# A down product that walks its chunk pairs in a rolling order, with partial sums added in DRAM

## The chip, the cores and the metric

The kernel runs on one core of a Trainium2 chip. The metric is the device time of one execution in microseconds. A core has a matrix engine (TensorE, PE in the profile; PEld is its weight load), a vector engine (VectorE, DVE), a scalar engine (ScalarE, ACT), a general engine (GpSimd, POOL), and a sync engine (SyncE, SP) that here only issues DMAs. Work memory is SBUF, TensorE writes to PSUM, and the large tensors lie in DRAM. A DMA can be issued by SP, ACT or POOL; each issuing engine starts its DMAs in its own program order.

## The reference

A trunk of two layers over 1024 tokens of 1024 channels, all in fp32. Each layer adds to the residual x a mixer, a cross-attention into 256 memory tokens, and a feed-forward block:

```python
def swiglu(h, w_gate, w_up, w_down):
    return (jax.nn.silu(h @ w_gate) * (h @ w_up)) @ w_down

x = x + swiglu(rms_norm(x, g_ffn[layer]), w_gate[layer], w_up[layer], w_down[layer])
```

The hidden width is 2816. The change concerns the last product, with w_down (2816 x 1024), and its addition to x, in both layers.

## The kernel before

**Layout.** Activations lie channel-major: a chunk is 128 channels by 1024 tokens. The hidden activations are 22 chunks, which the gate and up stage stores to the DRAM tensor pd. The residual has 8 chunks; between stages it lies in the DRAM tensor xs.

**Products.** Two neighbouring chunks form a Pair (lines 277 to 326), and its two chunks with the two halves of the tokens are a 2 x 2 block matrix; a Unit (lines 201 to 245) is the matching piece of a weight matrix, n pairs of 128-row blocks by 256 output channels. Seven products take the place of the eight of a 2 x 2 block product (function seven, line 1716): operand i of the unit and operand i of every pair, each a sum or difference of blocks. Each operand is kept as two numbers, a rounded high part (ScalarE, line 241 for weights, 318 for activations) and the rest (VectorE, line 409), so that a product takes three matmuls of 128 x 128 by 128 x 512 per pair (line 397): high by high, high by rest, rest by high. The sums and differences are made at line 232 for weights, on the engine named by the unit's argument adds, and at line 307 on POOL for activations. A unit of n pairs takes 7 splits (128n columns) and 4 sums; a pair takes 7 splits of 512 columns and 4 subtractions.

**Visits.** I call one unit with its pairs a visit. It accumulates in four PSUM banks and gives a quarter each for two output chunks. Its results go out in one of two ways: onto_x (line 1778) adds each product's bank to the resident residual chunk on VectorE, 8 adds per visit; collected (line 1741) builds the two output chunks in fresh tiles, by 3 ScalarE copies (lines 1756, 1762, 1764) and 4 VectorE adds (line 1754), and hands each quarter to a function. Gate and up use collected, the down product onto_x.

**The down product.** DOWN (line 32) splits the 11 chunk pairs into groups of 3, 3, 3 and 2. For each group the loop at line 1862 visits the four output pairs (of two chunks each, 256 channels), so a layer has 16 visits. The residual's 8 chunks are loaded from xs by x_back (line 1880), two of them in the gate and up stage and six in down_start (line 1841), into the "a" half of the raw arena, and stay there to the end. In the last group each finished quarter is passed on: in layer 1 to emit (line 2021), which transposes it on TensorE and stores it to the output; in layer 0, when a visit is done, to chunk_done (line 617), which normalises two chunks into the input of the odd mixer of layer 1 (lines 624, 625, 629, 632, 633). Its products (dense, line 665) then read chunk 0 first and chunk 7 last.

**Order of the work.** Every visit adds seven tasks with the operands they need. run (line 423) goes through the tasks and, ahead of each, fetches and makes operands of later tasks in the order of first use. Three numbers limit it: la, the columns made ahead of use; raws, the operand sources fetched and not yet begun; and f_reserve, which a unit's fetch must leave free in the raw arena. Raw data live in the F arena (16,384 columns, half "a" and half "b"), made operands in the R arena (35,840 columns); a buffer is reused once its last reader is done. A pair's chunks are loaded by SP from pd (line 1856) into "b" only, w_down by SP (line 222), also into "b" only. A tile scheduler then fixes each engine's program order from these priorities and its own timeline, and sets the waits.

Of the kernel before, what the change touches and what calls it, by code (L numbers as in the profile page):

```python
# [14 lines left out]
P = 128  # L15
S = 1024
# [15 lines left out]
DOWN = ((0, 1, 2), (3, 4, 5), (6, 7, 8), (9, 10))  # L32
# [244 lines left out]
class Pair:  # L277


    def __init__(self, load=None, home="ab", adds="gpsimd"):  # L280
        self.load, self.home, self.adds = load, home, adds
# [52 lines left out]
class Trunk:  # L334
    def __init__(self, tc, ctx, args):
# [48 lines left out]
        self.f_reserve = 0  # L384
        self.pS, self.pT, self.pM, self.pF = PSETS
# [231 lines left out]
    def chunk_done(self, gname, layer, k):  # L617
# [9 lines left out]
        if k == 0:  # L627
# [8 lines left out]
    def stats(self):  # L636
# [10 lines left out]
        self.ssq.free()  # L647

# [1092 lines left out]
    def collected(self, quarter, where="ba"):  # L1741
# [54 lines left out]
    def ffn(self, layer, pairs, finish=None, opening=None, emit=None):  # L1796
# [33 lines left out]

        self.add(start)
        for j in range(NF // 2):
# [14 lines left out]
        def down_end():  # L1847
            self.la, self.reserve = 3072, 0

        for n, group in enumerate(DOWN):  # L1850
            last = n == len(DOWN) - 1

            def load(f):
                def fn(t0, t1):
                    for e, t in enumerate((t0, t1)):
                        nc.sync.dma_start(out=t.ap, in_=self.pd[layer, (f + e) * P:(f + e + 1) * P, :])
                return fn
            home = "b" if last and finish else "ab"
            ps = [Pair(load(2 * j), home) for j in group]
            if last and opening:  # L1860
                self.add(opening)
            for mp in range(KD // 2):
                u = Unit(wd, group[0] * 256, len(group), mp * 256, "b", "b" if last and finish else "ba", "gpsimd")
                lead = [u.parts[0]] + [o for p in ps[:-1] for o in p.ops] if mp == 0 else ()
                if last and mp == 1:
                    self.add(down_end)
                quarter = None
                if last:
                    seen = []

                    def quarter(m, half, seen=seen):
                        if emit:
# [209 lines left out]
```

## Time and profile before

| | us |
|---|---|
| median of three runs | 2492.29 (2490.76 to 2493.66) |
| the profiled execution, its time | 2492.48 |
| its span on the core | 2490.7 |
| PE busy in the span | 2369.1 |
| DVE busy | 1722.8 |
| ACT busy | 1026.5 |
| POOL busy | 853.0 |

The mean granted TensorE clock was 0.973. The time of an execution lies 1.8 us over the span of its instructions. In the profile's names, arena_f and arena_r are the F and R arenas, psum_t is PSUM; a row of the grouped view reads: line, engine, operation, output<-inputs, output shape<-input shape, count, then busy us, mean ns of one, and the idle time of the engine just ahead of these, with what ended it. In the table of stretches each engine has its busy us and, in brackets, its instructions; then come the granted clock, the mean share of the 16 DMA engines in use, and GB/s. In the views of waits each row is: who waited, for whom, us in total, times, longest us.

### The profile page before, as it was taken

What the parts mean: (1) busy time and instruction counts of PE and PEld (TensorE: products, weight loads), DVE (VectorE), ACT (ScalarE), POOL (GpSimd) and SP (SyncE); (2) the same over time, 40 slices, a digit from 0 to 9 for tenths busy, and PEclk for the clock granted to TensorE, in tenths of its full rate; (3) what the DMA queues carried; (4) which work ended last, traced back from release to release, by engine and by line L of the source; (5) the groups of instructions that cost most, each with busy time, mean ns of one, the idle gap of its engine ahead of it and who ended that gap; (6) DMA issues with size and microseconds to landing.
All of it is one profiled execution on the core that took longest, in us unless ns stands there. A gap on an engine that the chain in (4) does not pass through costs nothing. (4 is left out here: it accounts for less than half of the span.)

```text
span 2490.7 us, 30370 instructions
## 1 busy us (share of the span) xinstructions
PE 2369.1 (95%) x11246; PEld 1978.2 (79%) x11246; DVE 1722.8 (69%) x2449; ACT 1026.5 (41%) x1886; POOL 853.0 (34%) x849
## 2 busy tenths in 40 slices
PE   7999999999899999998899999999799999989998
PEld 7998889888678888876677888888588887767776
DVE  5456367855686676689989643545876767589887
ACT  5355366645543333343335221244533333344332
POOL 6551233243531112136654300132721111146551
PEclk9999999999889999999999999999799999999999
DMA  7345345421231312243222121110321231243322
GB/s 233 124 144 172 94 119 141 132 76 35 102 102 51 102 60 85 93 139 110 93 89 81 60 59 35 59 43 18 118 85 68 93 102 51 74 164 102 102 87 74
DMA packets 175836, 234.83 MB, mean 94 GB/s; under 512 B 7200, under 2 KB 145528, under 8 KB 175688
## 3 DMA queue, kind: packets, MB, share of 16 engines
q1 hardware_dynamic: 171856, 220.10, 28.1%
q0 software_dynamic: 3648, 12.75, 1.4%
q8 instruction: 88, 1.44, 0.2%
q14 instruction: 60, 0.49, 0.1%
q10 hardware_dynamic: 184, 0.05, 0.0%
HBM read 176.11 MB, written 56.75 MB: 93 GB/s over the span
## 5 line engine op out<-in xcount | busy, mean ns | idle before, releaser
L397 PE MATMUL psum_t<-arena_r 128*128 128x512 f32 (+4 forms) x10304 | 2293.3, 381 | 99.1 <-DVE arena_r L409 43.4
L397 PEld LDWEIGHTS psum_t<-arena_r 128*128 128x128 f32 (+1 forms) x10304 | 1867.5, 191 | 473.9 <-DVE arena_r L409 67.1
L409 DVE TENSOR_TENSOR arena_r<-arena_f,arena_r 128x512 fp32r<-128x512 f32 (+4 forms) x839 | 739.0, 904 | 303.5 <-ACT arena_r L241 153.6
L241 ACT CAST arena_r<-arena_f 128x512 fp32r<-128x512 f32 (+2 forms) x532 | 288.8, 563 | 565.1 <-PE psum_t L397 402.3
L1806 POOL TENSOR_TENSOR arena_f<-arena_f 128x512 f32<-128x512 f32 x88 | 135.1, 1538 | 656.3 <-ACT arena_f L1805 656.1
L307 POOL TENSOR_TENSOR arena_f<-arena_f 128x512 f32<-128x512 f32 x120 | 184.1, 1550 | 120.4 <-DMA arena_f<-pd 58.2
L232 POOL TENSOR_TENSOR arena_f<-arena_f 128x384 f32<-128x384 f32 (+1 forms) x128 | 148.2, 1166 | 103.6 <-DVE arena_r L409 51.7
L1785 DVE TENSOR_TENSOR arena_f<-psum_t,arena_f 128x512 f32<-128x512 f32 x256 | 167.7, 680 | 15.7 <-PE psum_t L397 15.0
L318 ACT CAST arena_r<-arena_f 128x512 fp32r<-128x512 f32 x210 | 123.6, 617 | 124.9 <-POOL arena_f L307 62.4
L232 DVE TENSOR_TENSOR arena_f<-arena_f 128x512 f32<-128x512 f32 x176 | 136.0, 778 | 55.6 <-DMA arena_f<-w_up 34.2
L1754 DVE TENSOR_TENSOR arena_f<-psum_t,arena_f 128x512 f32<-128x512 f32 x176 | 119.9, 685 | 33.9 <-PE psum_t L397 28.3
L527 ACT CAST arena_r<-arena_f 128x1024 fp32r<-128x1024 f32 (+1 forms) x57 | 59.0, 1042 | 109.9 <-PE psum_t L397 99.5
L409 DVE TENSOR_TENSOR arena_r<-psum_t,arena_r 128x512 fp32r<-128x512 f32 (+3 forms) x124 | 84.7, 703 | 24.9 <-ACT arena_r L1596 8.7
L1805 ACT ACTIVATE arena_f<-arena_f 128x512 f32<-128x512 f32 x88 | 55.6, 632 | 99.7 <-DVE arena_f L1804 99.2
L633 POOL TENSOR_TENSOR arena_f<-arena_f 128x1024 f32<-128x1024 f32 x21 | 60.3, 2870 | 87.0 <-ACT arena_f L632 79.7
L1259 POOL TENSOR_SCALAR arena_f<-arena_f,small 128x640 f32<-128x640 f32 (+6 forms) x64 | 49.4, 780 | 108.6 <-DVE small L1258 104.6
L1813 DVE TENSOR_TENSOR arena_f<-arena_f 128x512 f32<-128x512 f32 x88 | 73.9, 841 | 3.3
L1804 DVE TENSOR_TENSOR arena_f<-arena_f 128x512 f32<-128x512 f32 x88 | 70.7, 804 | 0.8
L420 POOL TENSOR_TENSOR small<-small,mhalf 128x4 f32<-128x4 f32 (+1 forms) x64 | 64.3, 1005 | 5.2
L1705 POOL TENSOR_TENSOR arena_f<-arena_f 128x512 f32<-128x512 f32 x28 | 43.7, 1571 | 50.7 <-ACT arena_f L1704 50.2
L1948 POOL TENSOR_TENSOR arena_f<-arena_f 128x1024 f32<-128x1024 f32 x4 | 9.6, 2392 | 140.9 <-DVE arena_f L1900 136.1
L1254 ACT ACTIVATE arena_f<-psum_t,small 128x640 f32<-128x640 f32 (+6 forms) x64 | 47.5, 744 | 23.0 <-DVE small L1252 20.1
(177 smaller groups left out, 1390.9 us busy)
## 6 DMA issues: line engine op xcount, KB each, us to landing
arena_f<-w_gate SPq DMA_DIRECT2D x22, 1024.0 KB
arena_f<-w_up SPq DMA_DIRECT2D x22, 1024.0 KB
pd<-arena_f SPq DMA_DIRECT2D x44, 512.0 KB
arena_f<-pd SPq DMA_DIRECT2D x44, 512.0 KB
arena_f<-w_down SPq DMA_DIRECT2D x24, 768.0 KB
arena_f<-xs SPq DMA_DIRECT2D x32, 512.0 KB
arena_r<-qk SPq DMA_DIRECT2D x48, 256.0 KB
xs<-arena_f SPq DMA_DIRECT2D x24, 512.0 KB
```

The costliest lines, as they stand in the source:

```text
L232: getattr(T.nc, self.adds).tensor_tensor(out=out, in0=a, in1=b, op=what)
L241: T.nc.scalar.copy(out=hv, in_=src)
L307: getattr(T.nc, self.adds).tensor_tensor(out=out, in0=a, in1=b, op=ALU.subtract)
L318: T.nc.scalar.copy(out=h.ap, in_=src)
L397: self.nc.tensor.matmul(out=out, lhsT=lhsT, rhs=rhs, start=start, stop=stop, skip_group_check=again)
L409: getattr(self.nc, eng).tensor_tensor(out=out, in0=src, in1=high, op=ALU.subtract)
L420: self.nc.gpsimd.tensor_tensor(out=out, in0=in_, in1=self.mhalf[:, 0:in_.shape[-1]], op=ALU.pow)
L1754: nc.vector.tensor_tensor(out=o, in0=bank[q].ap, in1=o if other is None else other, op=ALU.add)
L1785: nc.vector.tensor_tensor(out=o, in0=bank[q].ap, in1=o, op=ALU.add)
L1804: nc.vector.tensor_tensor(out=q, in0=q, in1=r, op=ALU.mult)
L1806: nc.gpsimd.tensor_tensor(out=q, in0=q, in1=r, op=ALU.mult)
L1813: nc.vector.tensor_tensor(out=c[j].ap[:, o], in0=c[j].ap[:, o], in1=s.ap[:, o], op=ALU.mult)
```

## The change

The four fixed groups go. The visits now take the output pairs in turn: visit n (from -3) works on output pair n mod 4 and on the chunk pairs n to n+3, as far as they exist, so that each visit takes up one new chunk pair and lets go of one, and each chunk pair is met by all four output pairs in four visits running. In layer 1 that makes 14 visits of 1, 2, 3, eight times 4, 3, 2 and 1 pairs. In layer 0 only nine chunk pairs are rolled (visits of 1, 2, 3, six times 4, 3, 2 and 1 pairs), and four last visits take pairs 9 and 10 to the output pairs 1, 2, 3, 0.

A visit that isn't the last for its output pair collects its two chunks in fresh tiles and adds them onto xs in DRAM by a DMA with accum_op on POOL's queue, one per chunk. The last visit of an output pair adds onto the residual chunks as before; x_back loads these two chunks ahead of the last visits, one output pair at a time, in place of all eight at the start.

Moved along with this: the units of w_down no longer name "gpsimd" for their sums, so that Unit's default, VectorE, makes them; chunk pairs and most units may be loaded into both halves of the F arena, and a pair's fetch honours f_reserve too; la in the stage is 8192 (was 16384), f_reserve 4096 (was 0), raws 4 (was 2, set for gate and up). The first visit of a group no longer names operands of the whole group as its lead. chunk_done starts its sum of squares with whichever chunk comes first, since chunks 0 and 1 now come last in layer 0. collected takes its second tile at product 4, not at product 0.

```diff
     def fetch(self, T, must):                       # Pair
         if self.load is None:
             return True
+        if not must and sum(map(T.F.room, self.where)) - 3 * S < T.f_reserve:
+            return False
         got = []
         for cols in (S, S, 512, 512):
-            b = T.F.alloc(cols, "b")
+            b = T.F.alloc(cols, self.where)
...
             if i == 0:                              # collected
-                st["c"] = [self.F.get(S, where) for _ in range(2)]
+                st["c"] = []
+            if i in (0, 4):
+                st["c"].append(self.F.get(S, where))
...
+        rolled = 9 if finish else 11                # ffn
+        visits = [(n % 4, [j for j in range(n, n + 4) if 0 <= j < rolled]) for n in range(-3, rolled)]
+        if finish:
+            visits += [(mp, list(range(rolled, NF // 2))) for mp in (1, 2, 3, 0)]
...
-            if j == 9:
-                self.add(lambda: self.x_back(0, 2))
 
         def down_start():
             self.rbc.free()
-            self.x_back(2, KD)
-            self.la, self.f_reserve = 16384, 0
+            self.x = [None] * KD
+            self.la, self.f_reserve, self.raws = 8192, 4096, 4
         self.add(down_start)
...
+        ps = [Pair(load(2 * j), "b" if finish and j >= rolled else "ab", "gpsimd", "ba") for j in range(NF // 2)]
+
+        def onto_xs(m):
+            def fn(j, half, c):
+                if (j, half) in ((1, 0), (0, 1)):
+                    def keep():
+                        nc.gpsimd.dma_start(out=self.xs[(m + j) * P:(m + j + 1) * P, :], in_=c[j].ap,
+                                            accum_op=ALU.add)
+                        c[j].free()
+                    self.defer(keep)
+            return fn
...
-            for mp in range(KD // 2):
-                u = Unit(wd, group[0] * 256, len(group), mp * 256, "b", "b" if last and finish else "ba", "gpsimd")
...
+        for n, (mp, group) in enumerate(visits):
+            last = all(v[0] != mp for v in visits[n + 1:])
+            late = n >= len(visits) - 6
+            u = Unit(wd, group[0] * 256, len(group), mp * 256, "b" if late else "ba",
+                     "b" if finish and late else "ba")
...
+            if last:
+                nxt = [v[0] for v in visits[n:]]
+                if n + 4 == len(visits):
+                    self.add(lambda mp=mp: self.x_back(2 * mp, 2 * mp + 2))
+                if n + 1 < len(visits):
+                    self.add(lambda q=nxt[1]: self.x_back(2 * q, 2 * q + 2))
+                if n + 3 == len(visits):
                     self.add(down_end)
...
+            self.seven(u, [ps[j] for j in group], self.onto_x(2 * mp, last_part(mp)) if last else
+                       self.collected(onto_xs(2 * mp), "b" if late else "ba"))
```

More of the change, by code (lines that the diff above doesn't have):

```diff
@@ L31 @@
 AF_COLS = 16 * 1024
-DOWN = ((0, 1, 2), (3, 4, 5), (6, 7, 8), (9, 10))
 class Buf:
@@ L277, with __init__ @@
 class Pair:
-    def __init__(self, load=None, home="ab", adds="gpsimd"):
-        self.load, self.home, self.adds = load, home, adds
+    def __init__(self, load=None, home="ab", adds="gpsimd", where="b"):
+        self.load, self.home, self.adds, self.where = load, home, adds, where
         self.t = [None, None]
@@ L384, in __init__ @@
         self.f_reserve = 0
+        self.ssq = None
         self.pS, self.pT, self.pM, self.pF = PSETS
@@ L647, in stats @@
         self.ssq.free()
+        self.ssq = None
     def spread(self):
@@ new lines, in load, with fn @@
+        def load(f):
+            def fn(t0, t1):
+                for e, t in enumerate((t0, t1)):
+                    nc.sync.dma_start(out=t.ap, in_=self.pd[layer, (f + e) * P:(f + e + 1) * P, :])
+            return fn
[8 more added lines that the diff above has]
+                    self.defer(keep)
+            return fn
```

40 lines of the change are left out of this document (14 added, 26 removed).

## The prediction

> **What bounds the kernel now.** I read the page first, then a table of four stretches: 200 us out of each gate and up stage (800 to 1000, 1850 to 2050) and the two down products with what runs into them (1110 to 1376 for layer 0, 2223 to the end for layer 1).
>
> ```profile
> PE 2369.1 (95%) x11246; PEld 1978.2 (79%) x11246; DVE 1722.8 (69%) x2449; ACT 1026.5 (41%) x1886; POOL 853.0 (34%) x849
> ```
> ```profile
> core 0: us, PE busy (x) PEld busy (x) DVE busy (x) ACT busy (x) POOL busy (x), PEclk, DMA share, GB/s
> 800.00:1000.00 200.00, 199.38 (x880) 164.76 (x879) 141.10 (x201) 72.13 (x125) 32.25 (x22) 1.00 0.26 84
> 1110.00:1376.00 266.00, 238.46 (x988) 187.65 (x989) 243.84 (x325) 109.03 (x200) 152.55 (x109) 0.97 0.31 101
> 1850.00:2050.00 200.00, 199.03 (x879) 164.50 (x878) 136.87 (x190) 69.15 (x121) 30.47 (x20) 1.00 0.25 82
> 2223.00:2490.70 267.70, 232.79 (x980) 183.59 (x979) 229.17 (x317) 90.94 (x184) 128.05 (x101) 0.94 0.32 101
> ```
>
> Gate and up run at TensorE's own pace: 880 matmuls in 200 us, 0.227 us each. A down product has 44 visits-by-pair of 7 products and 3 matmuls, 924 matmuls, so 210 us. Layer 0's window holds 988 x 0.227 = 224.5 us of them (64 belong to the next layer's input projection) and lasts 266: 41.5 us are lost. Layer 1's holds 916 of 512 columns (208 us) and 64 transposes (8.7 us, below) and lasts 267.7: 51 us are lost, some 5 of them behind the last product. These 92 us are all there is to win. VectorE is busy 92% and 86% of these windows, against 70% in gate and up. The waits of TensorE, layer 0 and then layer 1, name it too:
>
> ```profile
> PE psum_t L397 <- DVE arena_f L1785: 13.1, 9, 2.9
> PE psum_t L397 <- DVE arena_r L409: 11.7, 10, 3.1
> ```
> ```profile
> PE psum_t L397 <- DVE arena_r L409: 13.0, 8, 3.5
> PE psum_t L397 <- DVE arena_f L1785: 12.8, 10, 2.9
> ```
>
> So the down stages are VectorE's. What it does there, by shape (layer 0, then two rows and the transposes of layer 1):
>
> ```profile
> L1785 DVE TENSOR_TENSOR arena_f<-psum_t,arena_f 128x512 f32<-128x512 f32 x128 | 83.8, 679 | 4.6 <-PE psum_t L397 4.4
> L409 DVE TENSOR_TENSOR arena_r<-arena_f,arena_r 128x512 fp32r<-128x512 f32 x77 | 73.4, 985 | 6.9 <-ACT arena_r L318 6.1 <-issue 0.8
> L307 POOL TENSOR_TENSOR arena_f<-arena_f 128x512 f32<-128x512 f32 x42 | 64.7, 1557 | 46.1 <-DMA arena_f<-pd 28.8 <-DVE arena_r L409 17.3
> L409 DVE TENSOR_TENSOR arena_r<-arena_f,arena_r 128x384 fp32r<-128x384 f32 x77 | 64.6, 869 | 4.2 <-ACT arena_r L241 4.1
> L232 POOL TENSOR_TENSOR arena_f<-arena_f 128x384 f32<-128x384 f32 x44 | 53.8, 1233 | 28.3 <-DMA arena_f<-w_down 20.5 <-DVE arena_r L409 6.9
> L625 DVE SCALAR_TENSOR_TENSOR arena_r<-arena_f,gc,arena_r 128x1024 fp32r<-128x1024 f32 x8 | 14.2, 1781 | 1.3 <-ACT arena_r L624 1.2
> L409 DVE TENSOR_TENSOR arena_r<-arena_f,arena_r 128x256 fp32r<-128x256 f32 x28 | 13.3, 496 | 4.0 <-ACT arena_r L241 4.0
> L409 DVE TENSOR_TENSOR arena_r<-arena_f,arena_r 128x1024 fp32r<-128x1024 f32 x5 | 8.1, 1617 | 0.0
> ```
> ```profile
> L409 DVE TENSOR_TENSOR arena_r<-arena_f,arena_r 128x512 fp32r<-128x512 f32 x73 | 70.6, 999 | 8.9 <-ACT arena_r L318 8.8
> ...
> L409 DVE TENSOR_TENSOR arena_r<-arena_f,arena_r 128x256 fp32r<-128x256 f32 x28 | 16.1, 619 | 0.4 <-ACT arena_r L241 0.4
> L2027 PE MATMUL psum_t<-ident,arena_f 128*128 128x128 f32 x64 | 8.7, 273 | 0.0
> ```
>
> Layer 0's VectorE rows sum to 257.4 us, yet it is busy 243.8: neighbours overlap at their ends, so I count 0.94 of a reported duration. The same 512-column split costs less in gate and up, where POOL is busy 16% of the time and not 57%, while adds that read PSUM cost 0.68 in both:
>
> ```profile
> L409 DVE TENSOR_TENSOR arena_r<-arena_f,arena_r 128x512 fp32r<-128x512 f32 x73 | 56.4, 775 | 34.7 <-ACT arena_r L241 34.6
> L1754 DVE TENSOR_TENSOR arena_f<-psum_t,arena_f 128x512 f32<-128x512 f32 x44 | 29.9, 684 | 12.5 <-PE psum_t L397 12.3
> L1756 ACT COPY arena_f<-psum_t 128x512 f32<-128x512 f32 x10 | 5.8, 582 | 2.6 <-DVE arena_f L1813 2.3 <-DVE arena_r L409 0.2
> ```
>
> The timeline shows why: one split with POOL quiet, then POOL's subtractions, then a split of the same size beside them; last two smaller splits with POOL quiet.
>
> ```profile
> 1101.96 0.68 DVE L409 TENSOR_TENSOR arena_r<-arena_f,arena_r 128x512 fp32r<-128x512 f32 x1
> ...
> 1106.35 4.66 POOL L307 TENSOR_TENSOR arena_f<-arena_f 128x512 f32<-128x512 f32 x3 [0.69 <-DMA arena_f<-pd]
> 1106.90 1.29 DVE L409 TENSOR_TENSOR arena_r<-arena_f,arena_r 128x512 fp32r<-128x512 f32 x1
> ```
> ```profile
> 1095.88 0.55 DVE L409 TENSOR_TENSOR arena_r<-arena_f,arena_r 128x384 fp32r<-128x384 f32 x1
> ...
> 1325.11 0.41 DVE L409 TENSOR_TENSOR arena_r<-arena_f,arena_r 128x256 fp32r<-128x256 f32 x1
> ```
>
> The Trainium skill, "SBUF — State Buffer", section "Who interferes with whom", says that a VectorE instruction with two SBUF inputs contends with a GpSimd instruction that reads SBUF, and one with a single SBUF input does not; these rows agree (0.68 to 1.29, against a steady 0.68). The same page's summary would have the work that clashes put off the critical engine, which speaks against this change: by it alone the moved weight adds are a loss of some 75 us on VectorE over both layers, an estimate from the counts below, with nothing given back.
>
> **The change part by part.** Weight adds: Unit's default puts the four adds of a unit on VectorE and takes them off POOL (L232 POOL, 53.8 us and a few narrow ones per layer). Evictions: a visit that isn't the last for its output pair does 4 PSUM adds and 3 ScalarE copies in place of 8 adds. ScalarE is 41% and 34% busy here and takes 30 to 36 copies of 0.58 per layer. Layer 0 has 12 such visits and 4 last ones, layer 1 has 10 and 4.
>
> POOL keeps 44 subtractions of 1.557 = 68.5 us per layer, 29% of some 235. Between 0.775 at 16% and 0.985 at 57% that makes a 512-column split 0.84 (bounds: those two ends). Against 0.68 alone it is a factor of 1.24; 384, 256 and 128 columns become 0.68, 0.51 and 0.33 (128 alone 0.27, on the line through the three sizes). Weight adds I price like splits.
>
> Layer 1: units of 4, 3, 2 and 1 pairs, 8, 2, 2 and 2 of them, 11 instructions each: 88 x 0.84 + 22 x 0.68 + 22 x 0.51 + 22 x 0.33 = 107.4; pair splits 77 x 0.84 = 64.7; PSUM adds 40 x 0.684 + 32 x 0.68 = 49.2. Sum 221 against 128 x 0.68 + 77 x 0.999 + 84 x 0.859 + 28 x 0.619 = 253 (0.859 is layer 1's 384-column mean, near the 0.869 shown). Layer 0, units 6, 2, 6 and 2: 111.4 + 64.7 + 54.6 = 231 against 250 by the rows above. VectorE is relieved by 32 and 19 us. At 0.775 the sums are 208 and 217; at 0.985, 251 and 261, that is 9 us more than before in all.
>
> Which engine then leads is a matter of the visit. Net of the 0.94: a full visit costs VectorE 18 x 0.79 + 4 x 0.64 = 16.8 us, and TensorE 4 x 21 x 0.227 = 19.1, so TensorE leads. At the ramp, visits of 2 and 3 pairs with one new pair each cost VectorE 13.4 and 15.1 against 9.5 and 14.3; with the first visit's last step I count 7 us of stall per layer. For full visits I add 3% of their TensorE time, 5 and 4 us, an estimate (gate and up lost 0.6 us of 200 with a freer VectorE).
>
> Loads: before, chunk loads used only the "b" half of the raw arena beside the resident residual, and SyncE sat on full buffers; the first load of layer 0's down product left when gate and up were nearly done:
>
> ```profile
> SPq L222 <- DVE arena_r L409: 90.5, 14, 15.0
> SPq L1856 <- DVE arena_r L409: 84.7, 15, 12.5
> ```
> ```profile
> 1102.67 0.80 SPq L1856 DMA_DIRECT2D arena_f<-pd  x2
> ```
>
> With both halves in use I expect the entry's wait for chunks to go; the 7 us above are what is left. The residual's eight reloads move from the entry to the last four visits; the first pair is asked for just ahead of its visit, with a first product of 4 x 3 x 0.227 = 2.7 us as cover. The trace gives no landing for that queue; by POOL's 5.1 (below) 2.4 us stick out, taken for both layers, bounds 0 and 7.3.
>
> Accumulating DMAs: 24 and 20 of 512 KB on POOL's queue, each with a wait for the last PSUM add of its tile; behind it on POOL stand the next pair's subtractions. Nearest rows are the plain writes to the same tensor at the start, and their queue (35 us of 16 engines for 12.75 MB, 1.4 us per 512 KB):
>
> ```profile
> L734 POOL DMA_DIRECT2D xs<-arena_f x8: 929/968/1011, 13.3 to 62.2; - x8
> ...
> DMA to landing us min/median/max: 4.0/5.1/7.3
> ```
> ```profile
> q0 software_dynamic: 3648, 12.75, 1.4%
> ```
>
> Issue: 2 x 0.97 us of POOL per 19 us visit beside 6.2 us of subtractions: hidden by POOL's idle time; uncovered it would be 44 x 0.97 = 43 us. Moving: doubled for reading back, 2 x 2.8 us of the engines per visit, 0.30 on a share of 0.31: hidden, nothing on the path. An accumulate itself isn't in the trace; bounds are one plain write and, from a rival below, 9.5 us.
>
> Ends. Layer 1's last visits of 3, 2 and 1 pairs cost VectorE 13.4, 11.7 and 9.8 against TensorE's 16.5, 11.7 and 7 with the transposes: 2 us, as weights are made ahead; then the same 5 us tail. Layer 1: 210 + 8.7 + 7 + 5 + 2.4 + 2 + 5 = 240 against 267.7: 28 less.
>
> Layer 0's last four visits (two new pairs, two chunks normalised per visit) cost VectorE 14 x 0.79 + 4 x (11 x 0.48 + 8 x 0.64 + 2 x 1.78 x 0.94) = 66 us against 38 on TensorE. 17 of the 28 can be made ahead (5 of slack in the three visits before, 12 of the six full ones, within 8192 columns): 11 are left. And the odd layer's products read chunk 0 first, which now finishes last:
>
> ```profile
> 1360.29 18.89 PE L397 MATMUL psum_t<-arena_r 128*128 128x512 f32 x82 [0.95 <-DVE arena_r L409]
> ...
> 1372.41 1.15 ACT L624 ACTIVATE arena_r<-arena_f,gc 128x1024 fp32r<-128x1024 f32 x1 [2.47 <-DVE arena_f L1785]
> ...
> 1373.60 1.28 DVE L625 SCALAR_TENSOR_TENSOR arena_r<-arena_f,gc,arena_r 128x1024 fp32r<-128x1024 f32 x1
> ```
>
> Before, TensorE multiplied through that chain with 64 products of the next layer (14.5 us); now an add, L624 and L625 stand bare, 3 us. Layer 0: 210 + 7 + 4 + 2.4 + 11 + 3 = 237 against 266 - 14.5 = 251.5: 14 less.
>
> The sum is 28 + 14 = 42 off the profiled execution (span 2490.7, time 2492.48, the median being 2492.29): about **2451 us**.
>
> **The rivals.** First, VectorE stays the bound: the added adds meet POOL as often and the split stays at 0.985. Then only the entries gain:
>
> ```profile
> 1110.00:1137.00 27.00, 17.24 (x51) 11.00 (x51) 23.82 (x23) 9.94 (x18) 18.17 (x12) 0.87 0.51 183
> 2223.00:2245.00 22.00, 9.09 (x20) 4.58 (x19) 19.06 (x18) 7.44 (x13) 14.35 (x11) 0.70 0.56 193
> ```
>
> 51 and 20 matmuls, 11.6 and 4.5 us of work, took 27 and 22 us. Of these 33 us lost, half is VectorE's own work and stays; 17 less and 9 more give 2484. For it: five more two-SBUF instructions meet each POOL one. Against it: the timeline shows the stretch only beside POOL's work, and that halves.
>
> Second, slower: the accumulate. Two per visit follow one another on one queue and hold their tiles; if one takes over 9.5 us, two outlast a 19.1 us visit and the visits go at the queue's pace. At 12 us the 22 visits lose 4.9 each, 108 us, less the 42 won: 2558. For it: it reads and writes memory, and no row prices it. Against it: a plain one lands in 5.1 and many overlap; it would have to be twice as slow with no overlap.
>
> Third, TensorE runs free in both layers (split near 0.775, everything made ahead, layer 0's 11 us gone too): 42 + 11 + 14 (two ramps) + 9 = 76 less, 2416.
>
> **How the numbers follow.** Forecast 0.64, first rival 0.16, second 0.12, third 0.08. The forecast's own range is 2430 to 2472: its stalls doubled, or halved. Holding 8 in 10 it reaches over most of the first rival, 2428 to 2486; what is left out is the second, the third and a bit. 0.2% (5 us) is about what can be told from no change. Faster: forecast, third, and half of the first, 0.79; same 0.09; slower 0.12.
>
> **What would show it.** In the changed profile: 512-column splits in the down stages near 0.84 (0.98 means the first rival); POOL near 30% there; full visits of 84 matmuls in 19 to 20 us with TensorE's waits mostly in the first three and, in layer 0, the last four visits; TensorE bare for some us before the first odd product; accumulate landings under 9 us. Wrong it is if accumulates appear among the waits of the evictions, or if TensorE loses over 60 us in the two stages.

## The result, and the profile after

The changed kernel takes **2592.67 us** (median of four runs, 2585.44 to 2594.83) against 2492.32 for the kernel before, a ratio of 1.0398 (95% interval 1.0376 to 1.0419): 100 us slower, where 41 us faster was forecast. Its profiled execution took 2593.79 us with a span of 2592.0.

First the table of stretches, before and after, cut where gate and up end and where the odd mixer's input begins (as in the prediction: busy us and instructions of PE, PEld, DVE, ACT, POOL; then clock, DMA share, GB/s).

```profile
700.00:1110.00 410.00, 409.29 (x1803) 337.79 (x1801) 292.76 (x414) 154.97 (x269) 74.35 (x52) 1.00 0.26 87
1110.00:1390.50 280.50, 252.96 (x1056) 199.24 (x1057) 246.46 (x328) 109.03 (x200) 155.33 (x110) 0.98 0.30 97
1803.00:2223.00 420.00, 410.84 (x1800) 336.52 (x1798) 298.15 (x415) 155.50 (x270) 81.32 (x52) 1.00 0.25 84
```

```profile
700.00:1128.00 428.00, 406.01 (x1762) 329.03 (x1761) 304.31 (x412) 150.98 (x266) 76.34 (x50) 1.00 0.23 77
1128.00:1457.40 329.40, 279.57 (x1083) 217.26 (x1081) 236.08 (x347) 133.07 (x240) 106.81 (x72) 0.90 0.49 126
1869.00:2310.00 441.00, 411.33 (x1773) 330.54 (x1772) 314.79 (x422) 154.21 (x272) 87.60 (x54) 1.00 0.23 76
2310.00:2592.00 282.00, 247.12 (x1024) 193.72 (x1023) 206.27 (x302) 107.72 (x203) 80.80 (x59) 0.94 0.53 139
```

Two things went wrong, in different stages. Gate and up, which the prediction left untouched, lost 18 and 21 us (410 to 428, 420 to 441). The down products lost 49 and 14 us (280.5 to 329.4, 267.7 to 282) though VectorE got part of the relief that was forecast: it is busy 10 us less in layer 0 (236 in place of 246; 19 were forecast) and 23 less in layer 1 (206 in place of 229; 32 were forecast). It now stands idle for more than a quarter of both stages, so its own work no longer sets their length; the question is what does. The DMA share went from 0.30 to about 0.5 there.

**Gate and up.** TensorE's waits in these stages, after (layer 0, then layer 1):

```profile
PE psum_t L399 <- ACT arena_f L1769: 18.5, 16, 1.7
```
```profile
PE psum_t L399 <- ACT arena_f L1769: 21.7, 17, 2.5
```

L1769 is collected's last ScalarE copy, that of product 4. A layer's gate and up are 22 visits of 84 matmuls; 16 of them have this wait in layer 0 and 17 in layer 1. The timeline of after shows two of them, while before ran 377 matmuls with no gap over the same stretch:

```profile
781.10 19.33 PE L399 MATMUL psum_t<-arena_r 128*128 128x512 f32 x84 [0.97 <-ACT arena_f L1769]
802.14 19.47 PE L399 MATMUL psum_t<-arena_r 128*128 128x512 f32 x84 [1.71 <-ACT arena_f L1769]
```
```profile
774.73 85.62 PE L397 MATMUL psum_t<-arena_r 128*128 128x512 f32 x377
```

In the written instruction order, 33 products of gate and up now begin on the very PSUM bank that the product just ahead has left, so TensorE stands still until ScalarE has copied it out. The order is the tile scheduler's; why the later tile makes it choose so is not shown. Before there were six such places, and they had a row of their own in the waits of layer 1's gate and up:

```profile
PE psum_t L397 <- ACT arena_f L1764: 5.9, 6, 1.0
```

**The down products.** The waits of layer 0's down product after (1110 to 1410), VectorE's, ScalarE's and GpSimd's:

```profile
DVE arena_f L231 <- DMA arena_f<-w_down: 37.9, 11, 10.4
ACT arena_f L1761 <- DMA xs<-arena_f: 17.5, 4, 7.0
POOL xs L1869 <- DVE arena_f L1759: 61.0, 17, 13.0
POOL arena_f L308 <- DMA arena_f<-pd: 55.5, 9, 12.7
```

The weight sums on VectorE wait for w_down, the next visit's first copy waits for a tile that an adding DMA still reads, and GpSimd waits for a tile's last sum ahead of each adding DMA, and for chunks. A piece of the chain of waits in time order (start, us, what) joins these:

```profile
1201.82 0.69 DVE arena_f L1759
...
1203.72 5.38 DMA xs<-arena_f
1209.11 0.02 SPq L221
...
1209.23 8.99 DMA arena_f<-w_down
...
1218.32 0.69 DVE arena_f L231
```

The last sum of a partial result, the DMA that adds it to xs, then SyncE, which asks for a unit of w_down only now, because its place in the raw arena was held by the tile; 9 us later the weights are there. The timeline shows what stood still meanwhile:

```profile
1218.32 0.69 DVE L231 TENSOR_TENSOR arena_f<-arena_f 128x512 f32<-128x512 f32 x1 [10.38 <-DMA arena_f<-w_down]
1218.32 1.14 ACT L240 CAST arena_r<-arena_f 128x512 fp32r<-128x512 f32 x2 [11.48 <-DMA arena_f<-w_down]
1219.37 0.58 ACT L1767 COPY arena_f<-psum_t 128x512 f32<-128x512 f32 x1
1219.67 3.43 POOL L308 TENSOR_TENSOR arena_f<-arena_f 128x512 f32<-128x512 f32 x2 [11.78 <-DMA arena_f<-pd]
1220.00 12.65 PE L399 MATMUL psum_t<-arena_r 128*128 128x512 f32 x42 [4.75 <-ACT arena_f L1767]
1235.65 8.70 PE L399 MATMUL psum_t<-arena_r 128*128 128x512 f32 x30 [3.00 <-DVE arena_f L1759]
```

Three engines waited more than 10 us for loads. The copy L1767, which had to empty a PSUM bank, stood in ScalarE's order behind two roundings (L240) of weights that were not there, and TensorE waited 4.75 us for the copy. So a late load reaches TensorE as a late eviction.

### The profile page after: what moved, and what is told of

Read it like the earlier page. It is cut to its first block, busy times and chain, and to the rows that moved or that the text cites. A ratio compares the mean times of both kernels' runs of the same rounds, so it can differ in the third digit from the quotient of the medians.

```text
span 2592.0 us, 30399 instructions
## 1 busy us (share of the span) xinstructions
PE 2402.9 (93%) x11246; PEld 1990.0 (77%) x11246; DVE 1717.3 (66%) x2451; ACT 1059.9 (41%) x1938; POOL 763.5 (29%) x765
## 4 chain that ended last, share of the span: by engine, by line
PE 66%; DVE 11%; DMA 11%; issue 6%; POOL 3%; ACT 3%; SPq 0%; ACTq 0%; DVEq 0%; POOLq 0%
PE psum_t L399 63%; DVE arena_r L411 5%; DMA xs<-arena_f 3%; DMA arena_f<-w_down 2%; DVE arena_f L231 2%; DMA arena_f<-w_up 2%; DMA pd<-arena_f 2%; POOL arena_f L308 1%; DVE arena_f L1759 1%; DMA arena_f<-pd 1%; PE psum_t L1272 1%; ACT arena_r L240 1%; POOL arena_f L1708 1%; ACT arena_f L1769 1%; DVE arena_f L1818 1%
## 5 line engine op out<-in xcount | busy, mean ns | idle before, releaser
L399 PE MATMUL psum_t<-arena_r 128*128 128x512 f32 (+4 forms) x10304 | 2325.1, 384 | 165.2 <-ACT arena_f L1769 41.6
L411 DVE TENSOR_TENSOR arena_r<-arena_f,arena_r 128x512 fp32r<-128x512 f32 (+5 forms) x825 | 689.6, 858 | 327.5 <-ACT arena_r L240 160.6
L240 ACT CAST arena_r<-arena_f 128x512 fp32r<-128x512 f32 (+3 forms) x518 | 288.0, 573 | 582.0 <-PE psum_t L399 403.9
L1811 POOL TENSOR_TENSOR arena_f<-arena_f 128x512 f32<-128x512 f32 x88 | 138.5, 1580 | 683.0 <-ACT arena_f L1810 682.7
L231 DVE TENSOR_TENSOR arena_f<-arena_f 128x512 f32<-128x512 f32 (+3 forms) x296 | 226.5, 767 | 130.6 <-DMA arena_f<-w_up 60.0
L308 POOL TENSOR_TENSOR arena_f<-arena_f 128x512 f32<-128x512 f32 x120 | 199.5, 1682 | 196.1 <-DMA arena_f<-pd 88.0
L1759 DVE TENSOR_TENSOR arena_f<-psum_t,arena_f 128x512 f32<-128x512 f32 x264 | 179.6, 684 | 33.7 <-PE psum_t L399 16.5
L319 ACT CAST arena_r<-arena_f 128x512 fp32r<-128x512 f32 x210 | 126.5, 618 | 127.3 <-POOL arena_f L308 54.8
L1818 DVE TENSOR_TENSOR arena_f<-arena_f 128x512 f32<-128x512 f32 x88 | 98.2, 1116 | 6.2 <-DVE arena_f L1759 0.5
L411 DVE TENSOR_TENSOR arena_r<-psum_t,arena_r 128x512 fp32r<-128x512 f32 (+3 forms) x124 | 84.7, 703 | 24.6 <-ACT arena_r L1275 7.7
L1869 POOL DMA_DIRECT2D xs<-arena_f x44 | 39.2, 891 | 146.1 <-DVE arena_f L1759 127.5
L1262 POOL TENSOR_SCALAR arena_f<-arena_f,small 128x640 f32<-128x640 f32 (+6 forms) x64 | 49.6, 782 | 107.1 <-DVE small L1261 106.8
L1761 ACT COPY arena_f<-psum_t 128x512 f32<-128x512 f32 x66 | 38.6, 585 | 95.4 <-DVE arena_r L411 52.0
L1809 DVE TENSOR_TENSOR arena_f<-arena_f 128x512 f32<-128x512 f32 x88 | 65.9, 748 | 1.3
L1708 POOL TENSOR_TENSOR arena_f<-arena_f 128x512 f32<-128x512 f32 x28 | 43.1, 1553 | 50.5 <-ACT arena_f L1707 50.0
```

The source lines that it names most:

```text
L231: getattr(T.nc, self.adds).tensor_tensor(out=out, in0=a, in1=b, op=what)
L240: T.nc.scalar.copy(out=hv, in_=src)
L308: getattr(T.nc, self.adds).tensor_tensor(out=out, in0=a, in1=b, op=ALU.subtract)
L319: T.nc.scalar.copy(out=h.ap, in_=src)
L399: self.nc.tensor.matmul(out=out, lhsT=lhsT, rhs=rhs, start=start, stop=stop, skip_group_check=again)
L411: getattr(self.nc, eng).tensor_tensor(out=out, in0=src, in1=high, op=ALU.subtract)
```

## The experiments

All times below are single runs unless an interval is given. Single runs of the kernel before lay between 2484.6 and 2496.3 us, so a step of 10 us between two single runs is about what their scatter can make, one of 30 is not.

### The late second tile

The first theory for gate and up: it is the edit in collected, not the DMAs. tiles_at_start undoes it for gate and up (in the down product it stays, since the arena has no room for both tiles); late_tile_alone makes only this edit in the kernel before.

```diff
-                st["c"] = []
-            if i in (0, 4):
+                st["c"] = [self.F.get(S, where) for _ in range(1 if late else 2)]
+            if late and i == 4:
                 st["c"].append(self.F.get(S, where))
```

> The changed kernel with one part undone for gate and up alone: collected takes both tiles at product 0 again (the down product's visits still take the second at product 4). In the changed kernel TensorE lost 18.5 and 21.7 us in gate and up to the ScalarE copy of product 4 (L1769), some 1 us once per unit; gate and up grew from 410 and 420 us to 428 and 440. Theory A, the late second tile makes this: gate and up go back, about 2553 us. Rival: gate and up lose because other buffers or loads moved (the residual's early reload is gone, pairs use both halves of the raw arena): stays near 2592.

> The kernel before with this one part of the change alone: collected takes its second tile at product 4. Theory A: the same once-per-unit wait for the ScalarE copy appears in gate and up, 2492 + 38 = about 2530 us, and the down stages stay as before. Rival: 2492, nothing changes.

tiles_at_start took 2559.4 us, 34 less than the changed kernel (2553 was expected); late_tile_alone 2553.8, 61 more than the kernel before, where 38 more were expected. TensorE's waits in gate and up of layer 0, in the first and then in the second:

```profile
PE psum_t L399 <- DVE arena_f L1759: 0.3, 1, 0.3
```
```profile
PE psum_t L397 <- ACT arena_f L1766: 21.8, 16, 3.3
```

The sixteen waits for the copy come with the edit and go with it, so the cause is shown. Not settled is why the same edit cost 61 us alone and 34 in company, for the waits for the copy are alike (21.8 and 18.5 us in layer 0). Some of the difference lies in gate and up itself: between 700 and 1110 us late_tile_alone got 1663 matmuls done, the changed kernel 1699 and the kernel before 1803.

### The adding DMAs

From here on tiles_at_start (2559.4) is the base. no_adding_dma drops the DMAs, so the partial sums never reach the residual; plain_writes drops their adding, so only the last partial sum is left in xs; quarter_width_adds lets each carry 256 of its 1024 columns.

```diff
-                        nc.gpsimd.dma_start(out=self.xs[(m + j) * P:(m + j + 1) * P, :], in_=c[j].ap,
-                                            accum_op=ALU.add)
```

> Like tiles_at_start, and the adding DMAs are left out, so the partial sums of all visits but the last of an output pair never reach the residual. Theory B, the adding DMAs (31% of the 16 engines in the changed layer-0 down stage, 3.1 us of all engines each) make the chunk and weight loads late and hold the tiles: the down stages fall to what VectorE and TensorE need, about 2450 to 2470 us. Rival C, the loads are late because the raw arena with f_reserve frees buffers late and SyncE's queue is blocked behind that: near tiles_at_start, 2540 or more. Rival D, VectorE still sets the pace: 2510 to 2540.

> Like tiles_at_start, with the DMAs onto xs as plain writes (accum_op left out), so what is left in xs is the last partial sum and not the residual with all of them. Queue, waits and bytes written stay, the reading back goes. If the reading back is what costs (theory B by engine time), half or more of what no_adding_dma gains shows here: 2500 or lower. If it is the waits for landing and the order of POOL's queue, it stays within 10 us of tiles_at_start.

> Like tiles_at_start, but each adding DMA carries 256 of the 1024 columns, so three quarters of every partial sum never reach the residual. The number of DMAs, their issue, their waits and the order of the queues stay; bytes fall to a quarter. Theory B by engine time: the 86 us between tiles_at_start (2559) and no_adding_dma (2473) shrink to about a quarter, 2485 to 2505 us. Rival, the cost is in the number of DMAs, in their wait on POOL or in the fixed part of a landing: 2540 or more.

They took 2473.1, 2506.4 and 2513.5 us. The first is 3 us outside what was expected if the adding DMAs are the cause (2450 to 2470) and far from both its rivals, the second 6 us outside the same (2500 or lower), and the third lies between its two theories (2485 to 2505, and 2540 or more). Without the DMAs the kernel is 86 us faster than with them, and 19 faster than the kernel before. The same 280 us of layer 0's down product, in tiles_at_start and in no_adding_dma:

```profile
1110.00:1390.00 280.00, 232.20 (x912) 179.44 (x910) 207.50 (x302) 111.80 (x210) 88.34 (x67) 0.92 0.55 136
```
```profile
1110.00:1390.00 280.00, 247.44 (x1032) 197.54 (x1031) 229.07 (x324) 124.00 (x220) 81.69 (x48) 0.94 0.30 99
```

912 matmuls got done against 1032, at a DMA share of 0.55 against 0.30. VectorE's wait for w_down, again in this order:

```profile
DVE arena_f L231 <- DMA arena_f<-w_down: 33.8, 10, 7.8
```
```profile
DVE arena_f L231 <- DMA arena_f<-w_down: 9.0, 9, 2.2
```

SyncE's waits show the link. In tiles_at_start its loads of weights (L221) and chunks (L1861) stand behind adding DMAs; in no_adding_dma no wait for xs<-arena_f is left, and where a load still needs a collected tile's place it waits only for that tile's last sum (L1759):

```profile
SPq L221 <- DMA xs<-arena_f: 61.2, 6, 13.6
SPq L1861 <- DMA xs<-arena_f: 51.0, 7, 15.9
```
```profile
SPq L1861 <- DVE arena_f L1759: 33.8, 6, 8.0
...
SPq L221 <- DVE arena_f L1759: 31.6, 6, 7.7
```

TensorE's timeline in no_adding_dma at the place of the gaps shown above:

```profile
1149.62 58.58 PE L399 MATMUL psum_t<-arena_r 128*128 128x512 f32 x247 [4.05 <-DVE arena_r L411]
...
1226.75 73.07 PE L399 MATMUL psum_t<-arena_r 128*128 128x512 f32 x321 [0.26 <-DVE arena_f L1759]
```

plain_writes and quarter_width_adds left 33 and 40 us over no DMA at all, so the presence of the DMAs might cost something by itself: GpSimd waits in its order for the last sum of each tile, and the tiles are held until a landing. Two more kernels part these. one_row_adds sends one of 128 rows; pool_order_alone sends nothing, but GpSimd still waits for the last sum and does a short addition, behind which the tile is free.

```diff
-                        nc.gpsimd.dma_start(out=self.xs[(m + j) * P:(m + j + 1) * P, :], in_=c[j].ap,
+                        nc.gpsimd.dma_start(out=self.xs[(m + j) * P:(m + j) * P + 1, :], in_=c[j].ap[0:1, :],
                                             accum_op=ALU.add)
```
```diff
-                        nc.gpsimd.dma_start(out=self.xs[(m + j) * P:(m + j + 1) * P, :], in_=c[j].ap,
-                                            accum_op=ALU.add)
+                        nc.gpsimd.tensor_tensor(out=c[j].ap[:, 0:64], in0=c[j].ap[:, 0:64],
+                                                in1=c[j].ap[:, 64:128], op=ALU.add)
```

> tiles_at_start with each adding DMA cut to one row: it carries 1 of the 128 rows of its tile (4 KB in place of 512 KB), so 127 of 128 rows of each partial sum are left out of the result. The wait of GpSimd for the tile's last sum stays, the tile is still held until its DMA has landed, and the number of DMAs is the same; nearly all bytes and reading back are gone. Theory A (the bytes and the reading back hold the tiles and the DMA engines, and the loads on SyncE's queue stand behind them): most of the 86 us between tiles_at_start (2559) and no_adding_dma (2473) goes, so 2475 to 2485, and SyncE's waits for xs<-arena_f fall under 20 us in the first down product. Theory B (the presence of the DMAs in GpSimd's program order, each waiting for VectorE's last sum while the next pair's subtractions stand behind it, costs the 33 to 40 us that plain_writes and quarter_width_adds left): 2505 to 2515, about as quarter_width_adds (2513.5).

> no_adding_dma with a stand-in for the issue: where GpSimd issued the adding DMA it now adds 64 columns of the finished tile onto 64 others of it (a short instruction), and the tile is free right after; so the partial sums are left out of the result, as in no_adding_dma, but GpSimd still waits in its order for VectorE's last sum of each tile, with the next pair's subtractions behind it. Theory A (GpSimd's order makes the 25 us that one_row_adds still has over no_adding_dma): 2493 to 2500. Theory B (the 25 us come from tiles that are held for the DMA's landing, 4 to 5 us beyond the last sum, and loads of SyncE that stand behind that): 2473 to 2480.

| kernel | us | DMA to landing, median in layer 0 | time of the 16 engines on GpSimd's queue |
|---|---|---|---|
| no_adding_dma | 2473.1 | | |
| pool_order_alone | 2485.2 | | |
| one_row_adds | 2498.2 | 2.2 | 1.7% |
| plain_writes | 2506.4 | 3.2 | 3.9% |
| quarter_width_adds | 2513.5 | 3.3 | 3.4% |
| tiles_at_start | 2559.4 | 5.4 | 6.9% |

Read as a ladder: 12 us for GpSimd's order (with the short addition), 13 for issue and landing with next to no bytes, 8 for the bytes of a plain write, 53 for adding in place of writing. Each taken against the kernel before that was timed beside it, the steps are 8, 19, 6 and 53. The first three are each about the scatter of single runs; together they are 33, which is more. one_row_adds came out between its two theories (2475 to 2485, and 2505 to 2515), and pool_order_alone between its own (2473 to 2480, and 2493 to 2500), so GpSimd's order and the landing share the small part, with no clear winner. The large part is the adding. Its price in engine time is in the queue's rows of plain_writes and tiles_at_start:

```profile
q0 software_dynamic: 9984, 35.82, 3.9%
```
```profile
q0 software_dynamic: 9984, 35.82, 6.9%
```

For the same bytes, 3.9% of 2504.6 less the 35 us of the kernel before is 63 us, 1.4 for each of 44 DMAs; 6.9% of 2557.6 less 35 is 141 us, 3.2 each. Adding takes 2.2 times the engine time and lands 2.2 us later, and an issue takes 0.87 us of GpSimd in place of 0.55. Which of these makes the 53 us, the engines' time, the longer hold of the tile or the longer issue, is open: no kernel here changed one without the others. SyncE's waits do not settle it. For adding DMAs its loads of weights and chunks wait 112 us in tiles_at_start, 96 in plain_writes and still 90 in one_row_adds, which was expected to fall under 20 and is 61 us faster all the same; quarter_width_adds, slower than one_row_adds, has 39. So these waits show the link, but their sum is not its price. What drops with the large step is VectorE's wait for w_down in this stretch: 33.8 us in tiles_at_start, 13 to 18 in the three kernels with lighter DMAs, 9.0 without any.

### VectorE's sums and the rolling order

The prediction's middle step was that VectorE is relieved although w_down's sums move to it, since ScalarE takes part of the evictions and two-input instructions get cheaper when GpSimd is quieter. vector_adds_alone makes that edit alone in the kernel before, and vector_adds_timed is the same kernel measured with an interval; pool_adds_again takes it back in tiles_at_start.

```diff
-                u = Unit(wd, group[0] * 256, len(group), mp * 256, "b", "b" if last and finish else "ba", "gpsimd")
+                u = Unit(wd, group[0] * 256, len(group), mp * 256, "b", "b" if last and finish else "ba")
```

> The kernel before with this one part of the change alone: w_down's sums on VectorE and not on POOL. By the prediction's prices POOL falls from 57% to some 29% busy in the down stages, a 512-column split from 0.985 to 0.84 us, and VectorE gains 41 us of sums against 28 us of cheaper splits: 14 us more per layer, in all 2492 + 15 to 28 = 2507 to 2520. Rival (no relief from POOL): splits stay at 0.98, some 2560. Other rival (the sums were late on POOL, L241 waited for them): faster, 2480.

> The kernel before with one edit: w_down's sums on VectorE in place of GpSimd (the same as vector_adds_alone, now timed in rounds). The single look gave 2481.8 beside 2489.5. Theory A (the price of VectorE's two-input instructions in SBUF falls by more than the added sums cost): 2478 to 2486, faster by 0.3%. Theory B (the look was an outlier, as the prediction's weight of 75 us more VectorE work says): 2489 or above.

> Like tiles_at_start, with w_down's sums back on POOL. If the DMAs bound the stage (theory B), VectorE's load hardly matters: within 12 us of 2559. If VectorE bounds it (rival D), splits go back to 0.98 and the sums leave VectorE, net some 10 us less VectorE per layer: 2540. If POOL's queue bounds it, where the adding DMAs wait for VectorE with sums behind them: 2580 or more.

The edit alone took 2481.8 us beside 2489.5, and with an interval 2482.0 against 2490.3, a ratio of 0.9964 (0.9951 to 0.9978): 8 us faster, a small gain. By the prediction's prices it should have been a loss (2507 to 2520); the time is near the rival in which the sums had been late on GpSimd (2480). Taking the edit back in tiles_at_start cost 14 us (2573.5), between what was expected with the DMAs as the bound (within 12) and with GpSimd's queue (2580 or more), and not far above the scatter. The rows of vector_adds_timed for layer 0's down product, with GpSimd now busy 84 of 266 us and not 153:

```profile
L409 DVE TENSOR_TENSOR arena_r<-arena_f,arena_r 128x512 fp32r<-128x512 f32 x77 | 69.6, 931 | 5.2 <-ACT arena_r L318 4.4 <-PE psum_t L397 0.8
L409 DVE TENSOR_TENSOR arena_r<-arena_f,arena_r 128x384 fp32r<-128x384 f32 x77 | 44.2, 596 | 0.0
L232 DVE TENSOR_TENSOR arena_f<-arena_f 128x384 f32<-128x384 f32 x44 | 27.9, 645 | 0.0
```

The 384-column splits fell from 869 to 596 ns, and 64.6 us to 44.2; that and 4 us on the wider splits pay 24 of the 34 us that the 384- and 256-column sums now take. So VectorE is busier than before (254.6 us in place of 243.8), and yet the kernel is faster. TensorE's wait for VectorE's evictions in this stretch fell from 13.1 us to

```profile
PE psum_t L397 <- DVE arena_f L1785: 1.8, 2, 1.5
```

What pays for the other 10 us and for the gain is open. That the weights no longer stand in GpSimd's order behind its subtractions would fit; no run shows it by itself.

rolling_alone keeps the residual resident, adds every visit onto it on VectorE and has no adding DMA; only the visits go in the new order, with GpSimd's sums and la at 8192. rolling_vector adds VectorE's sums to it.

```diff
-        for n, group in enumerate(DOWN):
+        rolled = 9 if finish else 11
+        visits = [(n % 4, [j for j in range(n, n + 4) if 0 <= j < rolled]) for n in range(-3, rolled)]
...
-                self.seven(u, ps, self.onto_x(2 * mp, quarter), lead)
+            self.seven(u, [ps[j] for j in group], self.onto_x(2 * mp, last_part(mp) if last else None))
```

> The rolling order alone on the kernel before: residual resident in the a half, every visit adds onto it on VectorE, no adding DMA, no collected tiles, w_down's sums on POOL, raw data in the b half only (la 8192 in the stage). VectorE's work is that of before, one new pair per visit in place of three at a group's start. Prediction's reasoning: half of the 33 us lost at the two entries goes, 3 to 6 us come at the odd layer's start: about 2480 us. Rival: units of four pairs and a pair fill the b half (5632 of 8192 columns), so loads come late in every visit: 2510 or more.

> rolling_alone (visits in the rolling order, the residual resident, every visit adding onto it on VectorE, no adding DMA, two tiles not needed) with w_down's sums on VectorE too. If the two parts add up: 2493 less 8 to 14, so 2479 to 2485, no better than vector_adds_timed, since with the resident residual the raw data still come into the second half of the raw arena alone. If VectorE, with 8 sums per visit, four more sums per unit and 4 pairs per unit, is the bound that the rolling order makes worse: 2500 or more.

rolling_alone took 2493.0 beside 2489.5, no gain, between the 2480 of the prediction's reasoning and the rival's 2510; rolling_vector 2482.8, a ratio of 0.9969 (0.9958 to 0.9980), as expected, the same as VectorE's sums alone. With the residual resident and raw data in one half of the arena, the order of the visits is worth nothing by itself. Both kernels with VectorE's sums beat the kernel before and the changed one.

## Why the prediction was wrong, step by step

Undone one after the other, the parts are 34 us for the late tile, 86 for the adding DMAs, and 19 gained by the rest: 101 lost in all, from 2492.3 to the profiled 2593.8. That they add up is no proof, since each is the step from one kernel to the next, and in another order they can come out otherwise, as the late tile's 61 us alone show.

**What bounded the kernel.** The prediction's "So the down stages are VectorE's" is not shown. In vector_adds_timed VectorE is busier than before and the kernel faster, so its busy share was no proof. With VectorE relieved and no adding DMA the kernel is at 2473.1, inside the stated range (2428 to 2486), but 19 faster and not 41, and that is a kernel in which saving the partial sums costs nothing. The moved sums alone are worth 8 us in the kernel before; the copies on ScalarE, both halves of the arena and the new la, f_reserve and raws have no run of their own.

**The price of VectorE's instructions** was about right in the changed kernel: "0.84" was forecast for a 512-column split, layer 1 has 872 ns, and the grouped view of layer 0's down stage has

```profile
L411 DVE TENSOR_TENSOR arena_r<-arena_f,arena_r 128x512 fp32r<-128x512 f32 x116 | 93.7, 838 | 11.5 <-ACT arena_r L319 7.4 <-ACT arena_r L240 2.5 <-PE psum_t L399 1.6
```

with GpSimd at 106.8 of 329.4 us, 32%, near the 29% forecast. But in no_adding_dma, where the same work stands closer together, it is 908 ns at 29%, so the line from GpSimd's share to a price is rough. The first rival's 0.985 did not come. The rule of the Trainium skill, "SBUF — State Buffer", section "Who interferes with whom", that a two-input instruction of VectorE and GpSimd's reads of SBUF hold each other up agrees with the runs (a 384-column split takes 869 ns beside a GpSimd that is busy 153 of 266 us, 596 beside one that is busy 84). From the summary of the same page of the Trainium skill the prediction worked out a loss of 75 us with nothing given back; the move alone gained 8 us, and in layer 0 cheaper splits gave back 24 of the 34 us that the sums took.

**Accumulating DMAs: the step that failed most.** "Moving: doubled for reading back, 2 x 2.8 us of the engines per visit, 0.30 on a share of 0.31: hidden, nothing on the path." The 2.8 was nearly right (6.6% of 2592.0 is 171 us, less 35 is 136, 3.1 for each of 44), the "nothing on the path" wrong by 86. Two errors are in it. A mean share hides what happens in short pieces: of 4 us each in the same stage of after,

```profile
1182.00:1186.00 4.00, 4.00 (x20) 3.30 (x19) 4.00 (x5) 2.74 (x7) 2.70 (x3) 1.00 0.00 0
1211.00:1215.00 4.00, 4.00 (x19) 3.19 (x17) 0.00 (x0) 0.00 (x0) 0.00 (x0) 1.00 1.04 242
```

the share is 0 in the one and full in the other, just while the w_down load of the chain above was under way, with two chunk loads issued right behind it (1209.67) and another adding DMA issued at 1207.03. And the transfer was priced as traffic alone, not as a hold on its source: until it has landed, the tile cannot take the next load, and SyncE's loads stand in order behind it. The chain above shows both at work; how the 86 us divide between them is open, as said.

**The slower rival** had the right part and the wrong mechanism. It asked for 9.5 us per DMA, at which the visits would go at the queue's pace. The landings are far below ("many overlap", said of the plain writes, was not to be read from their row: the eight left 5 to 12 us apart and landed in 4.0 to 7.3):

```profile
DMA to landing us min/median/max: 5.1/5.6/8.6
```

It comes to 2558 us, by chance near tiles_at_start. The threshold gave a false safety: an adding DMA need not fill a visit to cost time; it is enough that loads wait for its tile. Of the prediction's own signs, "accumulate landings under 9 us" came true and told nothing, while "accumulates appear among the waits of the evictions" (the ScalarE row above, 17.5 us) told it. The other sign of being wrong, over 60 us lost by TensorE in the two stages, came true too: in layer 0 alone 1083 matmuls, 246 us at 0.227, took 329.4.

**Gate and up** were not in the sum at all. The change to collected was told in the description of the change, but its working never asked what taking the second tile at product 4 does where collected was in use already. It cost 34 us. The row of six waits of 1.0 us for the same copy would have given the price of one, and 33 of them come to some 33 us; that there would be 33 was to be seen only in the changed kernel's instruction order.

**Loads.** "With both halves in use I expect the entry's wait for chunks to go": it did not go. In no_adding_dma the first chunk load leaves at 1078.62, 24 us earlier than before (1102.67; a load of w_down had left at 1079.24 there), and yet TensorE has the gaps shown under Ramp. GpSimd waited 55.5 us for chunks in layer 0 after against 28.8 before, and 59.8 in no_adding_dma; but it waits 79.9 in vector_adds_timed, where only the sums have left it, so this wait grows with GpSimd's free time and says little of the loads. The other half of the arena is no longer the residual's, but the collected tiles live there too. For the residual's reloads 2.4 us per layer were forecast; SyncE stood 43.9 us at them (L1908) behind adding DMAs in layer 0 of the changed kernel, and what that cost TensorE no run shows.

**Ramp.** 7 us of stall per layer were forecast. In no_adding_dma, layer 0, TensorE's first visits read

```profile
1139.88 2.35 PE L399 MATMUL psum_t<-arena_r 128*128 128x512 f32 x9 [1.02 <-DVE arena_r L411]
1143.26 0.73 PE L399 MATMUL psum_t<-arena_r 128*128 128x512 f32 x2 [1.03 <-DVE arena_r L411]
1145.07 0.50 PE L399 MATMUL psum_t<-arena_r 128*128 128x512 f32 x1 [1.08 <-ACT arena_r L319]
```

and with the 4.05 us ahead of 1149.62 that is 7.2 us of gaps; two more just ahead of these rows, 2.61 us for a rounding (L319) and 2.02 for a split (L411), make it 11.8, more than half as much again as forecast. The clock was 0.89 between 1110 and 1149.6, so these 39.6 us held 102 matmuls, 23 us at 0.227: 16 us lost.

**Ends.** Layer 1 gained 20 us in no_adding_dma against 28 forecast, measured from the start of its gate and up to the end (687.8 to 667.8); layer 0 lost 2.4 (690.6 to 693.0) where 14 less were forecast. The trace says where the missing 16 us of layer 0 lie: the ramp lost 16 us where 7 were forecast, and the end, from 1299 to 1366.5 with the four extra visits, held 185 matmuls (42 us) and lost 25, at a clock of 0.87, where 11, 3 and 2.4 were forecast. The full visits between lost 4 us, as forecast (642 matmuls, 146 us, in 149.4). Why the two ends lost that much was not taken apart by a run.

## What to carry to other kernels

Price an added DMA three ways: its time on the engines, its place in the issuing engine's order, and how long it holds its source tile, and then ask which load stands in order behind that tile; a mean DMA share of 0.3 or even 0.6 doesn't show that it is hidden. Go through every user of a shared helper when a change edits it, and look in the profile before for the wait that the edit can multiply, however small its row. If a change bundles an idea with several side edits, time the side edits alone: here the one-word edit that moves the sums was worth 8 us by itself, another side edit cost 34, and the adding DMAs of the idea itself 86.

## What the runs showed of the hardware

An adding DMA to DRAM takes 2.2 times the engine time of a plain one of the same 512 KB (3.2 against 1.4 us of the 16 engines) and lands in 5.4 against 3.2 us; its issue takes 0.87 against 0.55 us of GpSimd (tiles_at_start and plain_writes).

Gaps of TensorE are paid twice if they are long. After the gap of 4.75 us that ends at 1220 the granted clock in the changed kernel is half for 4 us, and full after 8; after one of 3.00 us that ends at 1235.65 it is 0.60 over 4.3 us; after the gaps of 0.97 us in gate and up it is full at once:

```profile
1220.00:1224.00 4.00, 4.00 (x9) 3.14 (x10) 4.00 (x4) 1.77 (x4) 3.10 (x2) 0.50 0.00 1
1224.00:1228.00 4.00, 4.00 (x15) 3.19 (x14) 4.00 (x3) 3.75 (x8) 3.44 (x3) 0.74 0.54 73
1228.00:1232.60 4.60, 4.60 (x21) 3.53 (x19) 4.60 (x7) 0.94 (x2) 1.61 (x1) 1.00 0.86 244
1235.70:1240.00 4.30, 4.30 (x12) 3.40 (x13) 4.30 (x6) 0.96 (x2) 2.12 (x2) 0.60 0.91 294
```
```profile
781.10:785.00 3.90, 3.90 (x17) 3.25 (x18) 3.19 (x6) 1.07 (x2) 0.00 (x0) 1.00 0.00 2
```

9 and 15 matmuls in 8 us where 35 would fit: some 2.5 us on top of the 4.75. The Trainium skill, "TensorE: Matmul & The Clock Gate", Part 1 on the clock gate, says that the clock is halved after an idle window of about 3.4 us and comes back after as long a busy one; the rows of the longer gap agree. The one of 3.00 us is shorter than that window and was followed by a slow clock all the same, and the measurement decides. In layer 0's down stage this is no small part: of the 49 us lost, TensorE was busy 26.6 more (252.96 to 279.57) for 27 more matmul records, which account for 6; so some 20 us are slower matmuls, at a clock of 0.90 in place of 0.98, and the rest waits.
